# First loads of x from ScalarE's queue, a split last accumulation, and one warming matmul less in a two-layer hybrid decoder trunk

## The chip, the cores and the metric

The kernel runs on one core of one Trainium2 chip. The metric is the device time of one execution in microseconds (us), the median of three runs. Besides that there is one profiled execution with its trace; all rows below are from it. TensorE (PE) does the matmuls, VectorE (DVE) and ScalarE (ACT) the elementwise work, GpSimd (POOL) a few small operations, and SyncE (SP) issues the loads and stores.

## The reference

Two layers work on x of 256 tokens by 1024 channels, in float32. A layer is a token mixer and a feed-forward block, each followed by a layer norm over a scaled residual:

```python
proj = x @ w_in                                     # 1024 -> 4768 columns
q_lat, kv_lat, k_rope, ... = split(proj)            # 384 + 256 + 32 "latent" columns among them
y_rnn = gelu(g_rnn) * rg_lru(causal_dwconv(x_rnn, conv_w, conv_b), ...)   # a scan over the tokens
y_mla = mla_attention(q_lat, kv_lat, k_rope, ...)   # 16 heads, causal
mix = (sigmoid(gate_a) * y_rnn + sigmoid(gate_b) * y_mla) @ w_out
x = layer_norm(ALPHA * x + mix, ln1_g, ln1_b)
h_gate, h_val = split(causal_dwconv(x @ w_up, ffn_conv_w, ffn_conv_b))
x = layer_norm(ALPHA * x + (gelu(h_gate) * h_val) @ w_down, ln2_g, ln2_b)
```

## The kernel before

**Products.** Each float32 operand is split into a rounded part (hi, by ScalarE, L185 or L199) and the rest (lo, by VectorE, L186 or L200). `mm3` (L193) makes three matmuls of a product: hi by hi (L194), hi by lo (L195), lo by hi (L196). TensorE's instructions stand in the order of the program text. The order on every other engine is drawn up by a planner that estimates when each instruction can start; within an engine that order is then fixed.

**Start.** `WARM` = 8 matmuls of a zero tile (L209) run before there is data. `x_block` (L220) loads one or two of the eight 128-channel chunks of x (128 KB each) and splits them; five calls bring all of x. Between them stand the loads of the latent weights, four blocks `lat` of 672 KB (tile `raw`, L156), each split into `wh` and `wl`. All are issued by SP, in program order: x chunk 0 (x0), block 0 in three pieces (168, 168 and 336 KB), x chunk 1 ahead of the third piece, then x chunks 2 and 3 together, block 1 in two pieces of 336 KB, x 4 and 5, block 2, x 6 and 7, block 3; behind them the constants `cst`, the parameters `par` of both layers, the positions `posi` and the next weights (block g0 of the gate projection first). The first accumulation (tile `latp`) takes 12 matmuls of 336 columns for each of the eight chunks. When `par` is there, GpSimd, ScalarE and VectorE make the decay rates from it (tile `lruw`, L329 to L343).

**End.** The down-projection accumulates into `dacc`, for each of two row tiles (128 tokens) two PSUM banks of 512 columns. `finish` (L360) closes row tile 0, starts its layer norm on VectorE (`LayerNorm.tile`, L392), closes the five last chunks of row tile 1 (first half of the columns, then the second), and starts the layer norm of row tile 1. For each half `tile` makes z = ALPHA * residual + sums (L400) and its statistics (L404); then come the mean and variance (L405), the inverse root on GpSimd (L407), two scaling passes (L411, L414) and the stores (L416).

Of the kernel before, what the change touches and what calls it, by code (L numbers as in the profile page):

```python
# [11 lines left out]
F32 = mybir.dt.float32  # L12
# [3 lines left out]
ALU = mybir.AluOpType  # L16

P = 128
# [30 lines left out]
)  # L49
HELD = 4  # L50
WARM = 8
LINE = 256
STEP = 8
KORD = (0, 1, 4, 5, 2, 3, 6, 7)
# [71 lines left out]
def trunk(ctx, tc, x_tok, x_chan, pos, wts, par, lnrow, consts, out):  # L126
    nc = tc.nc
    A = nc.scalar
    V = nc.vector
# [4 lines left out]
    tiny = ctx.enter_context(tc.tile_pool(name="tiny", bufs=2))  # L134
# [8 lines left out]
    def bank(name):  # L143
        return pp.tile([P, 512], F32, tag="pb", name=name)
# [48 lines left out]
    def mm3(o, lh, ll, rh, rl, start, stop):  # L193
        T.matmul(o, lhsT=lh, rhs=rh, start=start, stop=False)  # L194
        T.matmul(o, lhsT=lh, rhs=rl, start=False, stop=False)  # L195
        T.matmul(o, lhsT=ll, rhs=rh, start=False, stop=stop)  # L196

    def split2(hi, lo, src):
        A.activation(hi, src, AF.Copy)  # L199
        V.tensor_tensor(out=lo, in0=src, in1=hi.bitcast(F32), op=ALU.subtract)  # L200
# [6 lines left out]
    spare = bank("spare")  # L207
    for _ in range(WARM):
        T.matmul(spare[:, :P], lhsT=idle, rhs=idle, start=True, stop=True)  # L209
# [9 lines left out]

    def x_block(kc, n):  # L220
        src = x0[kc // 4][:, (kc % 4) * S:(kc % 4 + n) * S]
        nc.sync.dma_start(
            out=src.rearrange("p (c s) -> p c s", c=n),
            in_=x_chan[kc:kc + n].rearrange("c p s -> p c s"),
        )
        hi, lo = (v[:, (kc % 4) * S:(kc % 4 + n) * S] for v in xs[kc // 4])
        split2(hi, lo, src)

    x_block(0, 1)
    latw0.update(latent_weights(  # L230
        0, 0, step=LH, parts=((0, LH), (LH, LATW), (LATW, 2 * LATW)),
        between=lambda: x_block(1, 1)))
    for i in range(1, 4):
        x_block(2 * i, 2)
        latw0.update(latent_weights(0, i, step=LATW if i > 1 else LH,
                                    parts=((0, LATW), (LATW, 2 * LATW))))
# [6 lines left out]
        out=mask[:, P:], in_=mask[:, P:], pattern=[[-1, P]],  # L243
# [108 lines left out]
    def out_last(accs, t, n, wts_of, act_of, hc):  # L352
        for h, c in hc:
            hi, lo = wts_of(c)
            ah, al = act_of(c)
            mm3(accs[t][h], ah[:, t * P:(t + 1) * P], al[:, t * P:(t + 1) * P],
                hi[:, 512 * h:512 * h + 512], lo[:, 512 * h:512 * h + 512],
                False, c == n - 1)

    def finish(ln, accs, n, wts_of, act_of, late):  # L360
        out_last(accs, 0, n, wts_of, act_of, [(h, n - 1) for h in range(2)])
        ln.tile(0, accs)
        hc = [(h, c) for h in range(2) for c in range(n - late, n)]
        out_last(accs, 1, n, wts_of, act_of, hc[:-HELD])
        if not ln.last:
            ln.turn(0)
        out_last(accs, 1, n, wts_of, act_of, hc[-HELD:])
        ln.tile(1, accs)

# [8 lines left out]
    class LayerNorm:  # L378
# [10 lines left out]
            if not last:  # L389
                self.xs = [(slot("xhi", F32R), slot("xlo", F32R)) for _ in range(2)]  # L390

        def tile(self, t, accs):  # L392
            l, last = self.l, self.last
            z = big.tile([P, D], F32, tag="xres", name="z", bufs=4, align_bytes=LINE)
            st = tiny.tile([P, 2, 6], F32, tag="st", name="st")
            mv = tiny.tile([P, 2], F32, tag="mv", name="mv")
            rs = tiny.tile([P, 1], F32, tag="rs", name="rs")
            hs = [slice(512 * h, 512 * h + 512) for h in range(2)]
            for h in range(2):
                V.scalar_tensor_tensor(  # L400
                    out=z[:, hs[h]], in0=self.xres[t][:, hs[h]], scalar=ALPHA, in1=accs[t][h],
                    op0=ALU.mult, op1=ALU.add,
                )
                V.bn_stats(st[:, h], z[:, hs[h]])  # L404
            V.bn_aggr(mv, st.rearrange("p a b -> p (a b)"))  # L405
            V.tensor_scalar(out=rs, in0=mv[:, 1:2], scalar1=EPS, scalar2=None, op0=ALU.add)
            G.tensor_tensor(out=rs, in0=rs, in1=nhalf[:, 0:1], op=ALU.pow)  # L407
            g, b = self.gb
            if last:
                for h in range(2):  # L410
                    V.scalar_tensor_tensor(out=z[:, hs[h]], in0=z[:, hs[h]], scalar=mv[:, 0:1],  # L411
                                           in1=g[:, hs[h]], op0=ALU.subtract, op1=ALU.mult)
                for h in range(2):
                    V.scalar_tensor_tensor(out=z[:, hs[h]], in0=z[:, hs[h]], scalar=rs,  # L414
                                           in1=b[:, hs[h]], op0=ALU.mult, op1=ALU.add)
                    nc.sync.dma_start(out=out[t * P:(t + 1) * P, hs[h]], in_=z[:, hs[h]])  # L416
                return
            nmr = tiny.tile([P, 1], F32, tag="nmr", name="nmr")
            V.scalar_tensor_tensor(out=nmr, in0=mv[:, 0:1], scalar=-1.0, in1=rs,
                                   op0=ALU.mult, op1=ALU.mult)  # L420
            for c in (0, 256):
                V.tensor_scalar(out=z[:, c:c + 256], in0=z[:, c:c + 256], scalar1=mv[:, 0:1],
                                scalar2=rs, op0=ALU.subtract, op1=ALU.mult)
            A.activation(z[:, hs[1]], z[:, hs[1]], AF.Identity, scale=rs, bias=nmr)
            self.res.append(z)
# [84 lines left out]
    ends = (None, None)  # L510
    for l in range(DEPTH):
# [337 lines left out]
        later[0] = False  # L849
        ln = LayerNorm(l, 0, xres, False)  # L850
        finish(ln, oacc, 8, lambda c: ow[c], mer_of, 5)
        tp = [bank("upt") for _ in range(NB)]

# [85 lines left out]
        for j in range(NPAIR - LAG, NPAIR - 1):  # L939
            out_chunk(dacc, j, dw[j], hq[j], (0, 1) if j < NPAIR - LATE else (0,))  # L940
        ln = LayerNorm(l, 1, xres, l == DEPTH - 1)
        finish(ln, dacc, NPAIR, lambda c: dw[c], lambda c: hq[c], LATE)
        if l < DEPTH - 1:
            xs, xres = ln.xs, ln.res
            lat = []
            lacc = [[bank("latp") for _ in range(2)] for _ in range(NT)]
            for i, kc in enumerate(KORD):
                if i == 5:
                    ln.turn(1)
                    ends = ln.ends  # L950
# [113 lines left out]
```

## Time and profile before

| | us |
|---|---|
| median of 3 runs (lowest, highest) | 795.62 (795.12, 796.52) |
| the profiled execution's own time | 796.0 |
| its span, first to last instruction | 794.2 |
| TensorE busy | 781.1 (98% of the span) |
| VectorE busy | 649.7 (82%) |
| ScalarE busy | 508.8 (64%) |
| GpSimd busy | 10.9 (1%) |

Busy time is the time in which an engine has an instruction under way. TensorE's matmuls overlap, so a share of 98% says that it nearly always has work, not how fast it works. The execution's own time holds 1.8 us around the span.

### The profile page before, as it was taken

Reading aid. Unit: us, or ns where it says so; the run is one execution under the profiler, and the core shown is the slowest. Engines: PE = TensorE matmul, PEld = TensorE weight load, DVE = VectorE, ACT = ScalarE, POOL = GpSimd, SP = SyncE. Lnnn points to the kernel's source line nnn. Section 1 sums busy time; section 2 is a strip of 40 time slices with the busy share of each in tenths; the row PEclk is TensorE's granted clock in tenths of the full one; section 3 lists DMA queues with packets and bytes.
Section 4 is the critical chain, followed back from the end, with each engine's and each line's share of the span. In section 5 each row is a group of like instructions: output and inputs, shape, how many; then the busy total and the mean of one; then the engine's idle time right before and its main releaser. Section 6 shows DMA issues by size and latency. Waiting matters only on the chain.

```text
span 794.2 us, 14518 instructions
## 1 busy us (share of the span) xinstructions
PE 781.1 (98%) x5712; PEld 733.8 (92%) x5712; DVE 649.7 (82%) x1260; ACT 508.8 (64%) x910; POOL 10.9 (1%) x27
## 2 busy tenths in 40 slices
PE   8999999999999999999999999999999999999996
PEld 8999899878999999999899999998799999999994
DVE  5998889997699977767877886999877998677765
ACT  5765987783777565555474579688667765556540
POOL 1000000000000000000000000000000000000000
PEclk9999999999999999999999999999999999999998
DMA  8955436525457545535625554563615665646311
GB/s 303 349 198 213 146 113 242 200 68 202 160 205 273 201 174 217 187 123 210 248 73 204 184 178 141 177 214 120 212 62 199 256 228 201 224 163 208 107 54 54
DMA packets 26468, 144.76 MB, mean 182 GB/s; under 512 B 3360, under 2 KB 7072, under 8 KB 11808
## 3 DMA queue, kind: packets, MB, share of 16 engines
q1 hardware_dynamic: 26400, 143.84, 51.2%
q8 instruction: 45, 0.74, 0.4%
q14 instruction: 23, 0.19, 0.1%
HBM read 140.68 MB, written 1.05 MB: 178 GB/s over the span
## 4 chain that ended last, share of the span: by engine, by line
PE 89%; ACT 4%; DVE 3%; DMA 1%; issue 1%; SPq 0%; POOL 0%; DVEq 0%
PE proj L196 16%; PE proj L195 16%; PE proj L194 16%; PE dacc L195 6%; PE dacc L194 6%; PE dacc L196 6%; PE oacc L194 2%; PE oacc L196 2%; PE oacc L195 2%; PE sps L759 2%; PE yps L802 2%; PE ptp L787 1%; PE sps L757 1%; PE upt L196 1%; PE upt L194 1%
## 5 line engine op out<-in xcount | busy, mean ns | idle before, releaser
L196 PE MATMUL proj<-xhi,wl 128*128 128x256 f32 x1216 | 341.0, 280 | 1.3 <-DVE wl L186 1.3
L194 PE MATMUL proj<-xhi,wh 128*128 128x256 f32 x1216 | 341.2, 281 | 0.0
L195 PE MATMUL proj<-xlo,wh 128*128 128x256 f32 x1216 | 341.1, 281 | 0.0
L186 DVE TENSOR_TENSOR wl<-raw,wh 128x1024 fp32r<-128x1024 f32 (+5 forms) x226 | 241.6, 1088 | 47.2 <-ACT wh L185 46.6
L185 ACT ACTIVATE wh<-raw 128x1024 fp32r<-128x1024 f32 (+5 forms) x226 | 209.0, 953 | 99.8 <-PE proj L195 83.8
L196 PEld LDWEIGHTS proj<-xhi,wl 128*128 128x128 f32 x1216 | 229.0, 188 | 1.9 <-DVE wl L186 1.9
L194 PEld LDWEIGHTS proj<-xhi,wh 128*128 128x128 f32 x1216 | 229.1, 188 | 1.4
L195 PEld LDWEIGHTS proj<-xlo,wh 128*128 128x128 f32 x1216 | 228.7, 188 | 1.4
L905 DVE SCALAR_TENSOR_TENSOR u<-proj,par,u 128x255 f32<-128x255 f32 (+1 forms) x176 | 83.5, 479 | 37.6 <-ACT u L902 35.4
L902 ACT ACTIVATE u<-proj,par 128x256 f32<-128x256 f32 x88 | 49.1, 558 | 91.4 <-DVE u L905 71.4
L195 PE MATMUL dacc<-wsl,hh 128*128 128x512 f32 x192 | 75.1, 391 | 0.0
L194 PE MATMUL dacc<-wsh,hh 128*128 128x512 f32 x192 | 75.1, 391 | 0.0
L196 PE MATMUL dacc<-wsh,hl 128*128 128x512 f32 x192 | 75.0, 391 | 0.0
L186 DVE TENSOR_TENSOR wsl<-raw,wsh 128x1024 fp32r<-128x1024 f32 (+2 forms) x66 | 69.8, 1076 | 0.0
L185 ACT ACTIVATE wsh<-raw 128x1024 fp32r<-128x1024 f32 (+2 forms) x66 | 59.7, 938 | 0.0
L196 PEld LDWEIGHTS dacc<-wsh,hl 128*128 128x128 f32 x192 | 36.0, 188 | 7.8
L194 PEld LDWEIGHTS dacc<-wsh,hh 128*128 128x128 f32 x192 | 36.1, 188 | 6.4
L195 PEld LDWEIGHTS dacc<-wsl,hh 128*128 128x128 f32 x192 | 36.1, 188 | 6.2
L199 ACT ACTIVATE hh<-u 128x256 fp32r<-128x256 f32 x48 | 19.6, 408 | 13.7 <-DVE u L913 13.7
L194 PE MATMUL oacc<-wh,mhi 128*128 128x512 f32 x64 | 26.7, 417 | 0.0
L196 PE MATMUL oacc<-wh,mlo 128*128 128x512 f32 x64 | 25.2, 394 | 0.0
L195 PE MATMUL oacc<-wl,mhi 128*128 128x512 f32 x64 | 25.1, 393 | 0.0
(213 smaller groups left out, 1129.1 us busy)
## 6 DMA issues: line engine op xcount, KB each, us to landing
raw<-in_wts SPq DMA_DIRECT2D x114, 1024.0 KB, 4.8
raw<-in_wts SPq DMA_DIRECT2D x8, 832.0 KB, 5.1
gb<-in_lnrow SPq DMA_DIRECT2D x8, 512.0 KB, 7.4
raw<-in_wts SPq DMA_DIRECT2D x4, 672.0 KB, 4.0
raw<-in_wts SPq DMA_DIRECT2D x7, 336.0 KB, 7.1
raw<-in_wts SPq DMA_DIRECT2D x4, 512.0 KB, 4.7
xres<-in_x_tok SPq DMA_DIRECT2D x2, 512.0 KB, 6.0
k<-krot SPq DMA_DIRECT2D x8, 128.0 KB, 2.4
```

What stands on the lines that cost most here:

```text
L185: behind(A.activation(h, w, AF.Copy), after[0])
L186: lo_ins = V.tensor_tensor(out=lo[:, c - a:d - a], in0=w, in1=h.bitcast(F32), op=ALU.subtract)
L194: T.matmul(o, lhsT=lh, rhs=rh, start=start, stop=False)
L195: T.matmul(o, lhsT=lh, rhs=rl, start=False, stop=False)
L196: T.matmul(o, lhsT=ll, rhs=rh, start=False, stop=stop)
L199: A.activation(hi, src, AF.Copy)
L757: T.matmul(sps[:, :P], lhsT=q96[:, h4, :P], rhs=k96[:, h4, :P], start=True, stop=True)
L759: T.matmul(sps[:, P:P + S], lhsT=q96[:, h4, P:], rhs=k96[:, h4], start=True, stop=True)
L787: T.transpose(ptp[:, b * P:(b + 1) * P], sns[hh][:, b * P:(b + 1) * P], ident)
L802: T.matmul(yps[hh * 64:hh * 64 + 64, t * P:S], lhsT=vs[:, hv:hv + 64], rhs=pts[hh][:, 2 * t * P:(2 + t) * P], start=t == 0, stop=t == 1)
L902: ea = A.activation(dst, src, AF.Identity, scale=pcol(l, "fw", 96 + ch), bias=pcol(l, "fb", ch))
L905: ev = V.scalar_tensor_tensor(out=dst[:, k:], in0=src[:, :S - k], scalar=pcol(l, "fw", 48 * (2 - k) + ch), in1=dst[:, k:], op0=ALU.mult, o ...
```

## The change

Three edits. The five loads in `x_block` are issued on ScalarE's queue instead of SP's. In the last layer norm alone, the last `ENDS` = 3 of the five closing chunks of row tile 1's second half are cut in two by columns: columns 512 to 767 go into the old bank, columns 768 to 1023 into a bank of their own, `dend`. `LayerNorm.tile` then makes z of the whole half from the old bank (its last quarter without those three chunks), takes statistics of columns 512 to 767, adds `dend` to the last quarter, and takes that quarter's statistics; the aggregate reads three sets. And `WARM` is 7 instead of 8.

```diff
-WARM = 8
+ENDS = 3
+WARM = 7
...
     def x_block(kc, n):
         src = x0[kc // 4][:, (kc % 4) * S:(kc % 4 + n) * S]
-        nc.sync.dma_start(
+        nc.scalar.dma_start(
...
+    def out_split(accs, t, n, wts_of, act_of, late):
+        ends = bank("dend")[:, :256]
+        for dst, a in ((accs[t][1][:, :256], 512), (ends, 768)):
+            for c in range(n - late, n):
+                hi, lo = (w[:, a:a + 256] for w in wts_of(c))
+                ah, al = (x[:, t * P:(t + 1) * P] for x in act_of(c))
+                mm3(dst, ah, al, hi, lo, a == 768 and c == n - late, c == n - 1)
+        return ends
...
     def finish(ln, accs, n, wts_of, act_of, late):
         out_last(accs, 0, n, wts_of, act_of, [(h, n - 1) for h in range(2)])
         ln.tile(0, accs)
         hc = [(h, c) for h in range(2) for c in range(n - late, n)]
+        if ln.last:
+            out_last(accs, 1, n, wts_of, act_of, hc[:-ENDS])
+            ln.tile(1, accs, out_split(accs, 1, n, wts_of, act_of, ENDS))
+            return
         out_last(accs, 1, n, wts_of, act_of, hc[:-HELD])
-        if not ln.last:
-            ln.turn(0)
+        ln.turn(0)
...
-        def tile(self, t, accs):
+        def tile(self, t, accs, ends=None):
-            st = tiny.tile([P, 2, 6], F32, tag="st", name="st")
+            st = tiny.tile([P, 3, 6], F32, tag="st", name="st")
...
+            cuts = hs if ends is None else [hs[0], slice(512, 768), slice(768, 1024)]
             for h in range(2):
                 V.scalar_tensor_tensor(
                     out=z[:, hs[h]], in0=self.xres[t][:, hs[h]], scalar=ALPHA, in1=accs[t][h],
                     op0=ALU.mult, op1=ALU.add,
                 )
-                V.bn_stats(st[:, h], z[:, hs[h]])
-            V.bn_aggr(mv, st.rearrange("p a b -> p (a b)"))
+                V.bn_stats(st[:, h], z[:, cuts[h]])
+            if ends is not None:
+                V.tensor_tensor(out=z[:, cuts[2]], in0=z[:, cuts[2]], in1=ends, op=ALU.add)
+                V.bn_stats(st[:, 2], z[:, cuts[2]])
+            V.bn_aggr(mv, st[:, :len(cuts)].rearrange("p a b -> p (a b)"))
```

## Rows read from the trace of the kernel before

**Rows 1.** Busy time by stretch: stretch, length, each engine's busy us, clock, DMA share, GB/s.

```profile
0.00:4.50 4.50, 3.45 (x17) 3.45 (x17) 1.08 (x4) 2.18 (x3) 1.24 (x9) 1.00 0.55 137
4.50:8.00 3.50, 2.49 (x15) 2.18 (x14) 1.22 (x4) 1.66 (x4) 0.00 (x0) 1.00 0.94 315
8.00:22.00 14.00, 13.69 (x86) 13.06 (x85) 11.38 (x29) 9.65 (x20) 1.32 (x2) 1.00 1.00 371
...
60.00:130.00 70.00, 67.60 (x563) 66.73 (x562) 60.12 (x88) 53.74 (x80) 0.21 (x2) 1.00 0.52 179
```

**Rows 2.** The chain that ended last, from 0 to 40 us: start, length, what.

```profile
4.06 6.75 DMA raw<-in_wts
10.83 5.16 DMA par<-in_par
16.04 1.33 POOL lruw L329 x2
...
21.00 1.23 DVE wl L186
22.27 0.38 PE proj L196
```

**Rows 3.** Timeline of the first microseconds: start, length, instruction, idle time before and its end.

```profile
0.73 1.28 ACT L199 ACT_TABLE_LOAD   x1 [0.73 <-PEq L1053]
...
1.19 0.90 SPq L156 DMA_DIRECT2D raw<-in_wts  x2
...
2.93 0.42 ACT L199 ACTIVATE xhi<-x 128x256 fp32r<-128x256 f32 x1 [0.91 <-DMA x<-in_x_chan]
...
3.52 0.48 ACT L185 ACTIVATE wh<-raw 128x336 fp32r<-128x336 f32 x1 [0.18 <-DMA raw<-in_wts]
...
4.49 0.59 PE L194 MATMUL latp<-wh,xhi 128*128 128x336 f32 x1
...
7.78 0.42 PE L194 MATMUL latp<-wh,xhi 128*128 128x336 f32 x1 [1.01 <-ACT wh L185]
...
14.08 0.42 PE L195 MATMUL latp<-wl,xhi 128*128 128x336 f32 x1
```

**Rows 4.** DMA issues from 2.5 to 3 us: count, KB, us to landing.

```profile
raw<-in_wts SPq DMA_DIRECT2D x1, 336.0 KB, 4.6
```

**Rows 5.** Lines L209 and L757: ns min/median/max, first and last start.

```profile
L209 PE MATMUL spare<-idle x16: 421/421/579, 1.1 to 4.4; 128*128 128x128 f32 x16
...
L757 PE MATMUL sps<-k,q x64: 272/273/378, 129.8 to 558.3; 96*128 96x128 f32 x64
```

**Rows 6.** Timeline of the end, TensorE and VectorE.

```profile
769.73 0.28 PE L194 MATMUL proj<-xhi,wh 128*128 128x256 f32 x1
769.85 0.28 PE L195 MATMUL proj<-xlo,wh 128*128 128x256 f32 x1
...
784.63 0.74 DVE L414 SCALAR_TENSOR_TENSOR z<-z,rs,gb 128x512 f32<-128x512 f32 x1
...
785.30 0.68 DVE L404 BATCH_NORM_STATS2 st<-z 128x6 f32<-128x512 f32 x1
...
785.96 0.39 PE L195 MATMUL dacc<-wsl,hh 128*128 128x512 f32 x1
...
786.19 0.39 PE L196 MATMUL dacc<-wsh,hl 128*128 128x512 f32 x1
786.62 0.69 DVE L400 SCALAR_TENSOR_TENSOR z<-z,dacc 128x512 f32<-128x512 f32 x1 [0.64 <-PE dacc L196]
787.34 0.69 DVE L404 BATCH_NORM_STATS2 st<-z 128x6 f32<-128x512 f32 x1
788.07 0.21 DVE L405 BATCH_NORM_AGGREGATE mv<-st 128x2 f32<-128x12 f32 x1
```

**Rows 7.** VectorE's groups by shape: count, busy us, mean ns.

```profile
L186 DVE TENSOR_TENSOR wl<-raw,wh 128x512 fp32r<-128x512 f32 x32 | 20.9, 682 | 0.3 <-ACT wh L185 0.2
...
L809 DVE TENSOR_TENSOR mg<-yps,sB 128x256 f32<-128x256 f32 x16 | 6.7, 419 | 1.2 <-PE yps L802 1.2
```

## The prediction

> **What bounds the kernel now.** I read the page first: TensorE is busy for 781.1 of the 794.2 us, so an edit moves the time only where TensorE stands still. Busy time by stretch [rows 1] says where that is. From 0 to 8 us it is busy 5.94 us, part of that with warming matmuls; from 8 to 22 us it lacks 0.3 us; from 60 to 130 us it lacks 2.4 us, which no edit touches; and after its last product (786.6 us) it has 7.6 us of nothing, while the last layer norm and its stores run. The edits lie in the first and the last of these.
>
> The chain that ended last [rows 2] tells what the first pause costs. TensorE's last early stop ends at 22.27 us, when VectorE finishes the lo part of weight block g0 (21.00 to 22.23). VectorE came to that block late, because it first made the decay rates, and those hang on GpSimd at 16.04, which hangs on `par` landing at 15.99. `par` was issued at 10.83, when the second piece of latent block 1 landed (4.06 + 6.75 = 10.81). Counted in order of issue, that piece is the eighth transfer before it: I read this as at most eight transfers in flight. The DMA share is 0.94 and then 1.00 from 4.5 us on, at 371 GB/s from 8 us [rows 1]. So the date of `par` is set by the bytes ahead of it, not by SP's issuing. Stops before that one (7.78 and 14.08, [rows 3]) cost nothing of their own as long as TensorE reaches 22 us with its latent products done.
>
> At the end [rows 6] the chain is TensorE's last product (786.59), then z of the second half (786.62), statistics (787.34), aggregate (788.07), and from there a fixed sequence to the last store. VectorE is idle only from 785.98 to 786.62 there.
>
> **Loads of x on ScalarE.** Removed from SP: five issues at 0.45 us (two took 0.90, [rows 3]), 2.25 us in all. Added to ScalarE: five issues at about the same price, as nearest row. ScalarE stands free from 0.73, but it loads its function table then (1.28 us), under the line of the first activation. The load belongs to that activation, so issues that stand ahead of the activation stand ahead of the load. The five issues wait for no data, the activation does; I take all five to come first. Then: 0.73 + 2.25 + 1.28 = 4.26, hi of x0 to 4.68, hi of the first weights (0.48) to about 5.2. Before, the first products began at 4.49, straight behind the warming matmuls. So TensorE starts some 0.7 us later. Bound below: only x0's issue goes ahead, the table is there at 2.46, before x0 lands (2.93), the weights land 0.45 earlier, and the first product comes at about 4.06.
>
> The fourth and fifth issue may also have to wait for the first landing (eight in flight); queued behind them on ScalarE are the table load and both hi parts: at most 2.93 - 2.55 = 0.4 us more.
>
> The second chunk needs the third piece of block 0. Before, it was issued after 2.5 us, took 4.6 us [rows 4] and let TensorE go on at 7.78. Now SP issues it 0.95 us earlier, but x has a queue of its own that shares the same engines. If the two queues share equally, 672 KB of x have moved when that piece lands, where 256 KB had: 416 KB more, 1.15 us at 371 GB/s. If the transfers start 0.45 us earlier, the piece comes 0.7 us later, and chunk 1 starts at about 8.5, past the late start above (5.2 plus 12 products at 13.69/86 = 0.16 us is 7.1). That is why the late start costs nothing. For chunk 4 (stop at 14.08) the same count is 256 KB more, 0.7 - 0.45 = 0.25 later: 14.3, and four chunks of 1.9 us end at 21.9. The bytes ahead of `par` and g0 are the same, so these come 0.45 earlier and lo of g0 ends at 21.8. Both paths meet at 21.9 instead of 22.27: **-0.4 us**. Bounds: better, if the second queue fills the engines from 2 us on. By 8 us 137 x 4.5 + 315 x 3.5 = 1.72 MB had moved; at 371 GB/s from 2 us it would be 2.23 MB, which is 1.4 us. Worse: 0, if no transfer starts earlier and TensorE's products still end by 22, or a loss by the second rival below.
>
> **One warming matmul less.** It takes 0.43 us of TensorE (eight from 1.05 to 4.49) [rows 3, 5]. Nothing waits for it when data comes at 5.2: 0. What it covers is the clock. The record grants 1.00 throughout, yet these matmuls take 421 ns where a float32 matmul of the same 128 columns later takes 273 [rows 5], so I read them as running at the lower level (1.2 GHz) and the higher (2.4 GHz) as beginning with the first real products. That is priced as a rival.
>
> **The split last accumulation.** TensorE: nine matmuls of 512 columns become eighteen of 256. The pitch of the first is 786.19 - 785.96 = 0.23, of the second 769.85 - 769.73 = 0.12 [rows 6]: 2.16 - 2.07 = 0.1 us more, end at 786.68. The first nine end a microsecond before, at 785.6. VectorE is still on row tile 0's last pass and the first half's statistics then (784.63, 785.30, a pitch of 0.67 for 512 columns), so z of the second half can start at 785.97 and not before. From there by pitches: z to its dependent statistics 0.72 as now, statistics to aggregate 0.73; going from 512 to 256 columns takes 682 - 419 = 0.26 us off an instruction [rows 7]. So the third quarter's statistics start at 786.69, the added sum at 786.69 + 0.67 - 0.26 = 787.10, its statistics at 787.10 + 0.72 - 0.26 = 787.56, the aggregate at 787.56 + 0.73 - 0.26 = 788.03, against 788.07: **-0.04 us**. What VectorE gains by filling its pause it spends on two instructions more. TensorE's extra 0.1 us hides behind this: the added sum could start at 786.71 and starts at 787.10. Statistics of 256 columns have no row. If both cost as much as 512 columns, it is +0.5; if VectorE's order puts row tile 0's last pass behind, z starts at 785.65 and TensorE's end decides: -0.4. I take the rows' slope. The bank `dend` comes from a group last used by the up-projection, 12 us before, so nothing waits for it; the larger statistics tile costs the other layer norms nothing.
>
> **Sum.** -0.4 - 0.04, about -0.4 us. The profiled execution (796.0, span 794.2) would take 795.6 with a span of 793.8; it stands 0.4 above the median, so the median goes from 795.62 to **795.2**. Changes under 0.2% (1.6 us) are about what this measurement cannot tell from none.
>
> **Rivals.**
>
> *The engines fill (faster).* For it: from 0 to 4.5 us the DMA share is 0.55. Against: most of that is time before the first bytes, and the transfers in flight are many. With -1.4 at the start and -0.4 at the end: 793.8.
>
> *TensorE starts cold (slower).* Warming ends at 4.06, the first product comes at 5.2, and the higher clock, which began right with the first products before, may come later. A chunk then takes 3.8 instead of 1.9 us. The first is covered almost whole (5.2 + 3.8 = 9.0 against 8.5); each further one costs 1.9. It decides from the second on: three chunks end the products at 5.2 + 11.4 + 9.5 = 26.1, against 21.9; the stop would be 3.8 us later than now, and the time 799.4. With two chunks (24.2) it is 797.5. For it: the gap of 1.1 us that the edit opens. Against: a gap as long (6.8 to 7.78) was followed by products at full pace. The Trainium skill, TensorE: Matmul & The Clock Gate, What's actually happening, says that the throttled state is the default and activity releases it; by that rule fewer warming matmuls ahead of a gap speak for this rival, and the trace agrees in that the matmuls of the start are the slow ones.
>
> *ScalarE's issues undo the gain (no change).* The five issues and the wait on a landing take all that the freed queue gives; the stop stays at 22.27, the end at -0.04: 795.6. The Trainium skill, ScalarE: Activation LUTs, Table sets: the hidden batching unit, says that a pass puts a load before every activation that needs one; by that rule the table load stands behind x0's issue at least, and the trace has one load, right before the first activation's line. The sum of the late start is then the one above.
>
> *The planner's order changes elsewhere.* Other issue times can change the order on ScalarE and VectorE in the first layer, where TensorE lacks 2.4 us from 60 to 130 us. Losing or doubling that: 792.8 or 797.6.
>
> **Chances.** Forecast 0.50, undone 0.18, engines fill 0.14, cold 0.09, other order 0.09 (half each way). Faster by over 0.2%: most of the engines' case and a third of the other order, 0.14. Slower by over 0.2%: the cold case from two chunks on, and part of the other order, 0.09. Within 0.2%: 0.77. Range: from the engines' case, 793.8, to short of the cold one's two chunks, 797.0.
>
> **What would show it.** Right: ScalarE's table load near 3 us, first product near 5.2, stop on lo of g0 near 21.9, `par` landing near 15.5; at the end z of the second half straight behind the statistics of the first, and the aggregate about 1.35 us behind TensorE's last product (1.48 now, and that product 0.1 later). Wrong: a table load before 2 us, a first product near 4, products of the latent stage at 0.28 us pitch, or a new stop of TensorE between 22 and 130 us.

## The result and the profile after

The changed kernel takes 802.78 us (801.5 to 804.11, four runs) against 795.4 beside it: a ratio of 1.0086, 95% interval 1.0069 to 1.0103. A control later (six more runs) gave 801.16 against 796.49, 1.0059 (1.0047 to 1.0072). So the loss is 5 to 7 us, where the prediction had a gain of 0.4. One execution of a version below (the wider tile alone) took 851.05 us at a mean clock of 0.85; its number there leaves that one out, and its trace, which is of that execution, isn't used.

Its profiled execution has a span of 800.9 us, 6.7 more than before. Where they arise is seen by when the first and the last of the 1216 hi-by-hi products into `proj` start: 24.9 and 776.6 us now, 21.4 and 769.7 before. So 3.5 us are lost ahead of the first projection, 3.4 between, and 0.2 come back at the end.

Busy time by stretch, the same columns as [rows 1]:

```profile
0.00:4.50 4.50, 3.35 (x14) 3.06 (x14) 0.57 (x4) 2.11 (x4) 1.25 (x9) 1.00 0.59 186
4.50:8.00 3.50, 3.19 (x12) 2.66 (x12) 1.35 (x4) 0.82 (x2) 0.00 (x0) 1.00 0.98 313
8.00:22.00 14.00, 11.75 (x66) 11.39 (x67) 10.21 (x29) 8.14 (x18) 0.90 (x2) 0.88 0.91 327
60.00:130.00 70.00, 67.70 (x555) 67.10 (x554) 58.71 (x87) 52.53 (x78) 0.22 (x2) 0.98 0.49 173
92.00:95.40 3.40, 3.40 (x18) 3.40 (x18) 2.79 (x6) 3.37 (x7) 0.00 (x0) 0.51 0.76 251
```

From 8 to 22 us TensorE makes 66 matmuls, where it made 86 [rows 1], and two stretches lie at the lower clock: the mean granted clock is 0.88 in this stretch, and 0.51 from 92.0 to 95.4, which is the level of 1.2 GHz.

The timeline of the start, answering to [rows 3]:

```profile
0.73 1.38 ACTq L223 DMA_DIRECT2D x<-in_x_chan  x3
...
2.14 1.28 ACT L200 ACT_TABLE_LOAD   x1 [2.14 <-issue]
3.67 0.42 ACT L200 ACTIVATE xhi<-x 128x256 fp32r<-128x256 f32 x1 [0.24 <-DMA x<-in_x_chan]
...
4.51 0.65 PE L195 MATMUL latp<-wh,xhi 128*128 128x336 f32 x1
...
6.34 0.45 PE L197 MATMUL latp<-wh,xlo 128*128 128x336 f32 x1
...
6.62 0.32 PE L195 MATMUL latp<-wh,xhi 128*128 128x336 f32 x1
...
6.78 0.31 PE L196 MATMUL latp<-wl,xhi 128*128 128x336 f32 x1
...
7.38 0.32 PE L197 MATMUL latp<-wh,xlo 128*128 128x336 f32 x1
9.07 0.63 ACT L200 ACTIVATE xhi<-x 128x512 fp32r<-128x512 f32 x1 [3.70 <-DMA x<-in_x_chan]
9.61 1.59 ACT L186 ACTIVATE wh<-raw 128x336 fp32r<-128x336 f32 x4
...
10.12 0.65 PE L195 MATMUL latp<-wh,xhi 128*128 128x336 f32 x1 [2.42 <-ACT wh L186]
```

TensorE stops for 2.42 us (1.01 before, at 7.78 [rows 3]). What ends the stop is the hi of block 0's third piece (the first of the four at 9.61). That hi stands behind hi of x chunks 2 and 3 in ScalarE's order, and this one waits 3.70 us for its load. In the kernel before the third piece stood ahead.

The granted clock reads 1.00 up to 8 us, but the first products start at least 0.28 us apart, and only from 6.62 us on 0.15 to 0.16 (in the kernel before from 4.91 on). So the slow pace of the start is not in the mean clock of an execution.

DMA traffic from 2 to 9 us: queue (q1 is SP's, q10 ScalarE's), packets, MB, share of time:

```profile
q1 hardware_dynamic: 826, 1.66, 69.2%
q10 hardware_dynamic: 673, 0.64, 28.4%
...
x<-in_x_chan ACTq DMA_DIRECT2D x3, 256.0 KB, 7.4
```

x gets 45% of the packets, but 28% of the bytes: its packets carry 0.95 KB, SP's 2.0. The load of chunks 2 and 3, issued at about 1.65, takes 7.4 us and lands at 9.05. The third piece (336 KB, issued at about 1.65 too) takes 6.0 us and lands at about 7.6: it lay there for 2 us.

Further on, weight block g0 comes late as well (hi, lo, and its load, issued at 13.18):

```profile
20.88 2.01 ACT L186 ACTIVATE wh<-raw 128x1024 fp32r<-128x1024 f32 x2 [4.42 <-DMA raw<-in_wts]
...
21.98 1.23 DVE L187 TENSOR_TENSOR wl<-raw,wh 128x1024 fp32r<-128x1024 f32 x1 [1.44 <-ACT wh L186]
...
raw<-in_wts SPq DMA_DIRECT2D x1, 1024.0 KB, 7.6
```

In the kernel before this load, issued at 13.25, takes 5.9 us, and its hi starts at 19.25.

The end, VectorE, answering to [rows 6]:

```profile
792.17 0.69 DVE L420 BATCH_NORM_STATS2 st<-z 128x6 f32<-128x512 f32 x1
792.77 0.67 DVE L416 SCALAR_TENSOR_TENSOR z<-z,dacc 128x512 f32<-128x512 f32 x1
793.48 0.43 DVE L420 BATCH_NORM_STATS2 st<-z 128x6 f32<-128x256 f32 x1
793.82 0.40 DVE L422 TENSOR_TENSOR z<-z,dend 128x256 f32<-128x256 f32 x1
794.26 0.43 DVE L423 BATCH_NORM_STATS2 st<-z 128x6 f32<-128x256 f32 x1
794.72 0.24 DVE L424 BATCH_NORM_AGGREGATE mv<-st 128x2 f32<-128x18 f32 x1
```

z of the second half stands straight behind the statistics of the first, as forecast. From it to the aggregate it is 1.95 us (forecast 2.06).

### The profile page after: what moved, and what is told of

The parts are those of the page before. It is cut to its first block, busy times and chain, and to the rows that moved or that the text cites. A ratio compares the mean times of both kernels' runs of the same rounds, so it can differ in the third digit from the quotient of the medians.

```text
span 800.9 us, 14534 instructions
## 1 busy us (share of the span) xinstructions
PE 787.2 (98%) x5719; PEld 739.7 (92%) x5719; DVE 650.1 (81%) x1262; ACT 509.3 (64%) x910; POOL 10.5 (1%) x27
## 3 DMA queue, kind: packets, MB, share of 16 engines
q10 hardware_dynamic: 1104, 1.05, 0.4%
HBM read 140.68 MB, written 1.05 MB: 177 GB/s over the span
```

## The experiments

The theories: **order** (ScalarE's fixed order puts the third piece behind a late load), **address** (the wider statistics tile moves the buffers behind it), **warming** (one matmul less costs clock), and as rivals **bandwidth** (x gets too little on a queue of its own, whatever the order) and the **planner** (a new order of the other instructions). Ratios are to the kernel before, run beside each; they are estimates over all single executions, with a 95% interval, and not quotients of the two medians.

Single executions lie in steps by their mean granted clock. Of the 31 runs of the kernel before beside the last group of experiments, 14 have 0.997 and a median of 795.1 us, 14 have 0.995 and 796.8. Some comparisons below therefore look at times of equal clock.

### One part at a time

**Only the loads of x.** `nc.sync.dma_start` in `x_block` becomes `nc.scalar.dma_start`.

> The loads of x on ScalarE alone. Order theory (ScalarE's fixed order puts hi of x chunks 2 and 3 ahead of the third piece of latent block 0, and that load lands late on a queue of its own): TensorE stops until about 10 us, the clock falls behind that stop, and the time rises by 4 to 5 us, nearly all of the change's loss. Address theory (the wider statistics tile moves the buffers behind it and slows every product a little): only the early stop, 2 to 3 us, and the slow creep from 125 us on is gone. Warming theory (one matmul less sets the clock back): no stop of over 1.5 us and within 1 us of before.

798.46, ratio 1.0038 (1.0024 to 1.0051). TensorE stops for 2.24 us at 10.18, and the projections start at 25.1. The expected stop is there, and with it most of what is lost ahead of the projections. The loss of 2.4 us is what the address theory left for the loads (2 to 3); the order theory's 4 to 5 us, nearly all of the loss, was missed.

**Only the split end**, with the wider statistics tile.

> The split last accumulation alone, with its wider statistics tile. Order theory: the tail is shorter by 0 to 0.3 us and nothing else moves, -0.3 to +0.1 us. Address theory: the tail's gain and a creep of about 2 us over the run, so +1.5 to +2 us.

797.85, ratio 1.0024 (1.0015 to 1.0034): the second part that costs.

**Only `WARM = 7`.**

> Seven warming matmuls alone. Order theory: the first products wait for data as before, within 0.4 us of before. Warming theory: the clock rises one step later, the latent stage loses 1.5 to 3.5 us and the time rises by as much.

797.92, ratio 1.0023 (1.0013 to 1.0032). The edit alone also changes the planner's order on ScalarE and VectorE. The size is what the warming theory forecast, but ScalarE takes a copy of latent sums out of PSUM ahead of hi of g0:

```profile
20.13 0.45 ACT L487 ACTIVATE lat<-latp 128x336 f32<-128x336 f32 x1 [3.09 <-PE latp L196]
20.48 2.00 ACT L185 ACTIVATE wh<-raw 128x1024 fp32r<-128x1024 f32 x2
...
22.84 0.39 PE L196 MATMUL proj<-xhi,wl 128*128 128x256 f32 x1 [0.76 <-DVE wl L186]
```

In the unchanged kernel that hi starts at 18.95. In the changed kernel the order with seven and with eight is the same, so this price is not carried over.

**Control**: the kernel before.

> The kernel before, unchanged, as a control on the same chip. If the four single edits were really slower by 2 us each, this is within 0.1% of the runs of before, 795 to 797 us, with two groups 1.5 to 2 us apart by the mean granted clock (0.997 and 0.995). If the way of running makes the 2 us, this is at 798 too.

795.29, ratio 0.9998 (0.9988 to 1.0007).

The three parts sum to 1.0085, but warming counts there with an order that the whole change doesn't have; loads and split end alone give 1.0062.

### The warming matmul

**Seven and a short eighth** (16 columns), which keeps the kernel before's order:

```diff
-    for _ in range(WARM):
-        T.matmul(spare[:, :P], lhsT=idle, rhs=idle, start=True, stop=True)
+    for n in [P] * 7 + [16]:
+        T.matmul(spare[:, :n], lhsT=idle, rhs=idle[:, :n], start=True, stop=True)
```

> The kernel before with seven warming products of 128 columns and an eighth of 16 columns; the order of the instructions on every engine is the kernel before's, where the run with seven products alone had ScalarE's and VectorE's order changed near 20 us. Planner theory (what seven products cost was the changed order, which puts the first weight's hi behind a wait): 795.1 to 796.2, as the kernel before. Warming theory (the missing columns cost clock at the start): 797 to 798.5, and the stop behind the latent products stays at 0.76 us.

795.7, ratio 1.0001 (0.999 to 1.0012). The planner theory holds: what seven cost was the order, as far as 16 columns more make no difference.

**The changed kernel with `WARM = 8`:**

> The changed kernel with eight warming matmuls; no other instruction moves. Order theory: TensorE has a stop until 10 us either way, so within 0.5 us of the changed kernel (802.8). Warming theory: the clock stays up in more of the runs and it is 1.5 to 2 us faster, about 801.

801.16, ratio 1.006 (1.0047 to 1.0073). Seemingly 1.6 us better than 802.78, but the control of the changed kernel gave 801.16 as well:

> The changed kernel, unchanged, as a control with more runs and a second profile (there are only four runs of it so far). The parts as measured one by one: all of x on ScalarE's queue about 2.4, the moved buffers about 2.4, an additional stretch at half clock about 1.7 in those runs that have it. Sum theory: runs between 799.3 (mean clock 0.997 or above) and 803 (0.994), median 800.5 to 803. Rival (the four runs were high by the chip that they ran on): median below 800.

The sum theory holds: 801.16, ratio 1.0059. And the changed kernel with the third statistics set elsewhere (below) and eight products:

> The changed kernel with its third set of statistics in a slot and with eight warming products. Order of all instructions as in the version with the slot and seven (797.31). If the eighth product itself is worth something at the start (the changed kernel gained 1.6 from it): 795.5 to 796.8. If it is worth nothing and the 1.6 were the scatter of the clock's stretches: 796.9 to 798.8.

798.27, not better than 797.31 with seven. The eighth product is worth nothing that these runs can tell; the 1.6 us between the two results of the changed kernel are not its doing.

### The loads and the order

**x on ScalarE, with hi of the later chunks held behind the last hi of the weight block before:**

```diff
+                last_hi[0] = A.activation(h, w, AF.Copy)
...
-        split2(hi, lo, src)
+        behind(A.activation(hi, src, AF.Copy), last_hi[0])
+        V.tensor_tensor(out=lo, in0=src, in1=hi.bitcast(F32), op=ALU.subtract)
```

> The loads of x on ScalarE, with ScalarE's order held so that hi of x chunks 2 and 3 stands behind block 0's third piece. Order theory: the stop at 10 us shrinks from 2.2 us to under 0.6, the clock stays up behind it, and the run is 1.5 to 2.5 us faster than with the loads on ScalarE alone (798.5), so about 796 to 797. Bandwidth rival (x's own queue gets too little of the engines, whatever the order): the stop stays over 1.5 us, one chunk later, and the time stays at 798 or above.

798.75, ratio 1.0026 (1.0016 to 1.0036). The stop is gone, and the trace shows the third piece landing at 7.58; but later the gain is taken back:

```profile
7.58 0.86 ACT L186 ACTIVATE wh<-raw 128x336 fp32r<-128x336 f32 x2 [2.06 <-DMA raw<-in_wts]
...
8.11 0.42 PE L196 MATMUL latp<-wh,xhi 128*128 128x336 f32 x1 [0.47 <-ACT wh L186]
...
20.71 2.01 ACT L186 ACTIVATE wh<-raw 128x1024 fp32r<-128x1024 f32 x2 [4.24 <-PE latp L198]
...
23.08 0.39 PE L198 MATMUL proj<-xhi,wl 128*128 128x256 f32 x1 [0.76 <-DVE wl L188]
```

The projections start at 21.8, 3.3 us earlier than with the loads alone. But hi of g0 comes at 20.71 (18.95 in the control), TensorE stops at 23.08 for its lo, and this profile has a stretch at half clock near 90 us. The planner had also changed more of VectorE's order than with the loads alone. So order explains the stop at 10 us, but mending it brought back less than these runs can tell: 1.0026 against 1.0038, with intervals that overlap. The order theory's 796 to 797 was met by the three executions with a mean clock of 0.997 (median 796.85); the others lie higher, and the bandwidth rival's stop of over 1.5 us didn't come either.

**Only the first two loads of x on ScalarE**, the three of 256 KB on SP:

```diff
-        nc.sync.dma_start(
+        (nc.scalar if n == 1 else nc.sync).dma_start(
...
```

> The kernel before with only the first two loads of x (one chunk each, 128 KB) issued from ScalarE's queue, and the three larger ones left on SP's. Queue theory (a load of 1-KB rows beside weight loads of longer rows gets the smaller part of the engines, and SP's later issues wait for it): the two small ones land early as in the changed kernel (about 3.7 and 4.4 us), the 256-KB loads are as before, no stop near 10 us; 794.8 to 796.0, within 0.5 of the kernel before. Table-load theory (ScalarE's issues ahead of its table load are what costs): 797 or above.

794.56, ratio 0.9986 (0.9977 to 0.9994): a small gain, where the same edit on all five costs 0.38%. At a mean clock of 0.997 it is 0.45 us (794.54 against 794.99); the rest comes from the steps, for 9 of 11 executions have that clock here and 9 of 28 of the kernel before. What the 0.45 us are the profile doesn't show: its projections start at 21.0, the control's at 20.9. The 256-KB load of chunks 2 and 3 takes 5.5 us here (issued at 2.12, so it lands at 7.6), and there is no stop of TensorE over 0.15 us ahead of the gates.

### The statistics tile and where the buffers lie

`tiny`, the pool of the statistics, lies ahead of those of the weights, the large slots and the small tiles. A wider tile (two buffers, 32 bytes more each) moves the weight halves `wh`, `wl` by 64 bytes, the raw weights, the small tiles and `u` by 256, and the large slots (which hold hi and lo of x) not at all. That is read from the addresses in the built program.

**Only the wider tile**, `[P, 3, 6]`, third set never used; the order of all engines is the kernel before's.

> Only the statistics tile is wider (three sets of six, the third never used); the order on every engine is that of before. Order theory: within 0.3 us of before. Address theory: +1.5 to +2 us, as a creep over the two up-projection stages.

798.7 (six executions), ratio 1.0037 (1.0024 to 1.005). The address theory forecast this, but the tile's own work could cost as much; that is tried below.

**The split end with its three sets in a slot of the large pool**, the regular tile as before:

```diff
-            st = tiny.tile([P, 2, 6], F32, tag="st", name="st")
+            if ends is None:
+                st = tiny.tile([P, 2, 6], F32, tag="st", name="st")
+            else:
+                st = slot("st3")[:, :18].rearrange("p (a b) -> p a b", a=3)
```

> The split last accumulation with its three sets of statistics in a spare large buffer, so that the statistics tile keeps its size and no other buffer moves. Address theory: the creep over the up-projection stages is gone, 0.1 to 0.3 us faster than before, 1.5 to 2 us faster than the split with the wider tile (797.9). Rival (the split itself, or the run): it stays at 797.5 or above.

796.08, ratio 0.9999 (0.999 to 1.0009). The split itself costs nothing and gives nothing that the times can tell. The profiles can: from the start of the last hi-by-hi product into `proj` to the end of the span it is 24.5 us in every version without the split and 24.3 in every one with it.

**The changed kernel with that edit:**

> The changed kernel with one edit: the last row tile's three sets of statistics lie in a slot of the large pool, and the regular statistics tile has two sets again, as before. Order of all instructions as in the changed kernel. Address theory: the wider tile costs its 1.8 to 2.7 us here too; 800.0 to 801.2, and the product pitch of the late projections back at 117.8 ns from 118.9. Rival (the statistics tile costs only beside the early loads of the kernel before): 802 to 803.

797.31, ratio 1.0027 (1.0012 to 1.0041): 3.9 us below the control of the changed kernel, and about what the loads alone cost. That is more than the theory's 1.8 to 2.7: of the 4.2 us between the two profiles, 3.0 lie in the projections and 1.2 ahead of them, where this one has no stretch at half clock.

**The wider tile and an unused tile of 192 bytes**, so that all buffers behind move by 256 bytes together:

```diff
+    tiny.tile([P, 48], F32, tag="pad", name="pad", bufs=1)
```

> The kernel before with the wider statistics tile whose third set is never used, and an unused tile of 192 bytes beside it, so that all buffers behind lie exactly 256 bytes later, instead of the weights' halves 64 bytes later, the raw weights, the small tiles and u 256 bytes later, and the large slots not at all. The order of all instructions is the kernel before's. Address theory as an offset between buffers (the products slow down when the halves of the weights move against the large slots that they are multiplied with): no offset has changed, 795.1 to 796.5, as the kernel before. Rival (the tile itself costs: a longer row that VectorE writes and reads, or any move at all): 797.5 to 799, as with the wide tile alone.

795.32, ratio 1.0 (0.999 to 1.0011).

**An unused tile of 64 bytes at the head of the small pool**: the small tiles and `u` move as with the wider tile, the weights don't.

> The kernel before with an unused tile of 64 bytes at the head of the small pool: krot lies 64 bytes, the small tiles and u 256 bytes later, as with the wide statistics tile, and the weights' halves, the raw weights and the large slots stay. The order of all instructions is the kernel before's. If it is the weights' halves that cost (64 bytes against the large slots): 795.1 to 796.5. If it is the small tiles and u: 797.5 to 799.

796.37, ratio 1.0002 (0.9991 to 1.0012).

**The changed kernel with the 192 bytes:**

> The changed kernel with the same unused tile of 192 bytes, so that all buffers behind the statistics lie 256 bytes later than before the change and none has moved against another. Order of all instructions as in the changed kernel. Offset theory: 796.8 to 798.8, as with the third set in a slot of its own. Rival: 801 to 803, as the changed kernel.

798.36, ratio 1.0039 (1.0022 to 1.0056): 2.8 us below the control by the medians, with the width of the tile unchanged; but the eight executions lie apart, three at 800.9, as high as the control, and five at 796.5 to 798.5. The profiled one is of the three. Its projections take 748.6 us from the first to the last product, one stretch at half clock included; what it loses lies at the start:

```profile
16.04 0.46 PE L197 MATMUL latp<-wl,xhi 128*128 128x336 f32 x1
16.32 0.34 PE L198 MATMUL latp<-wh,xlo 128*128 128x336 f32 x1
16.50 0.32 PE L196 MATMUL latp<-wh,xhi 128*128 128x336 f32 x1
...
L196 PE MATMUL proj<-xhi,wh x1216: 276/280/415, 26.2 to 774.8; 128*128 128x256 f32 x174
```

Up to 16.32 us its products start at least 0.28 apart, only then 0.15, and the projections start at 26.2.

So it is neither the tile's work, nor any move, nor the small tiles: it is where the weights lie. The built program of the last run adds that the raw weights, the small tiles and `u` have the same addresses there as in the changed kernel; the halves lie 192 bytes later and the large slots 256. What is left is the place of the halves or of the raw weights against the large slots, or the halves' own place: they moved by 64 bytes with the wider tile alone, and by a whole 256, on which the raw weights and the slots are aligned, with the 192 bytes beside it. These were not tried apart. The line of the hi-by-hi products into `proj` (ns min/median/max, start of the first and the last) shows the cost, in order for the control of before, the wider tile beside 192 bytes, the split end with the wider tile, the changed kernel with the slot, and the changed kernel's control:

```profile
L194 PE MATMUL proj<-xhi,wh x1216: 276/281/370, 20.9 to 768.7; 128*128 128x256 f32 x174
```

```profile
L195 PE MATMUL proj<-xhi,wh x1216: 276/280/369, 21.5 to 769.1; 128*128 128x256 f32 x174
```

```profile
L195 PE MATMUL proj<-xhi,wh x1216: 274/281/368, 21.5 to 771.0; 128*128 128x256 f32 x174
```

```profile
L195 PE MATMUL proj<-xhi,wh x1216: 276/280/367, 23.8 to 770.9; 128*128 128x256 f32 x174
```

```profile
L195 PE MATMUL proj<-xhi,wh x1216: 274/281/367, 25.0 to 775.1; 128*128 128x256 f32 x174
```

From the first to the last it is 747.8, 747.6, 749.5, 747.1 and 750.1 us. The granted clock is 1.00 in all five over that time. The moved weights cost 1.7 to 1.9 us in the kernel before and 3.0 in the changed one, and no stop of TensorE is longer. By the starts in the traces, 1.7 of the 1.9 and 2.7 of the 3.0 lie in the products into `proj`, all of which read the halves; the products of the up-projection into `upt`, which read large slots alone, take the same. With the loads of x on ScalarE some halves also lie in other buffers of their pool (seen in the built programs), so the two prices need not be equal.

### The stretches at half clock, and the parts that held

Eight products of zeros fill the two stops of 0.99 us that the last gate chunk of layer 0 has in the kernel before (at 85.97 and 87.36 us), beside the split end with its statistics in a slot:

```diff
+                fill = 4 if l == 0 and c == 7 else 0
+                for _ in range(fill):
+                    T.matmul(ps[:, :P], lhsT=idle, rhs=idle, start=True, stop=True)
...
+                    for _ in range(fill if m == 0 else 0):
+                        T.matmul(o[:, :P], lhsT=idle, rhs=idle, start=False, stop=False)
```

> The split end with its statistics in a slot of their own (as in the run of that version, 796.08), and in layer 0 eight products of the idle tile (zeros, 128 columns) in the two stops of the last gate chunk: four ahead of its first product, four between its first and second, added into the open sum. About 0.2 us each against two stops of 0.99 us, so no product behind them should start later. Order of all other instructions as in that version. Clock theory: the two groups of times of the kernel before (795.1 with a mean clock of 0.997, 797.0 with 0.995) are one stretch at half clock behind these two stops; filled, no run shows it, nearly all runs lie at 0.997 or above, median 794.3 to 795.2, about 0.6 below the kernel before beside it. Rival (the stretch has another cause, such as the load on the chip): both groups stay, median 795.7 to 796.3. Second rival: the eight products delay the chunk, each of 0.2 us on the path, up to 1 us slower in the upper group.

795.23 (794.6 to 795.84, 11 runs), ratio 0.9993 (0.9984 to 1.0001). All 11 runs have a mean clock of 0.997 or above, where 18 of 28 of the kernel before beside it have 0.995. The clock theory holds; the gain in the median is on the edge of what can be told.

**Together**: this, and the first two loads of x on ScalarE.

> What held together: the first two loads of x from ScalarE's queue and the three larger ones from SP's, the split end with its statistics in a slot, eight warming products, and the eight products of zeros in the two stops of layer 0's last gate chunk. If the gains add (about 0.7 from the loads at equal clock, 0 to 0.1 from the split, and only the upper group of times): 793.8 to 794.8, 0.9 to 1.5 below the mean of the kernel before beside it. Rival (the filled stops move the low stretch elsewhere, or the start's gain is taken back behind the latent products): 794.9 to 796.

794.21 (793.88 to 794.76), ratio 0.998 (0.9971 to 0.9988). This beats both kernels. Stretches around the last gate chunk, columns as above, first in the run with 64 bytes in the small pool (the stops as they are), then in this one:

```profile
84.50:86.50 2.00, 0.68 (x3) 0.48 (x4) 2.00 (x4) 2.00 (x5) 0.00 (x0) 1.00 0.00 0
86.50:89.90 3.40, 3.40 (x18) 3.40 (x18) 2.79 (x6) 3.40 (x8) 0.00 (x0) 0.50 0.49 139
```

```profile
84.50:86.50 2.00, 1.90 (x15) 1.71 (x16) 2.00 (x3) 2.00 (x5) 0.00 (x0) 1.00 0.00 0
86.50:89.90 3.40, 3.40 (x32) 3.40 (x31) 2.78 (x6) 3.40 (x8) 0.00 (x0) 1.00 0.60 196
```

Eighteen products in 3.4 us against 32: at a pitch of 0.12 us, 1.7 us are lost in the one stretch, which is the step between the runs with 0.997 and 0.995.

## Why the prediction was wrong

**The loads, -0.4: the sign was wrong.** The step that failed is "the piece comes 0.7 us later, and chunk 1 starts at about 8.5". The piece did come (about 7.6), but the sum took it that ScalarE takes it as it lands. The planner writes ScalarE's order from its own idea of the landings, and it put hi of chunks 2 and 3 first. Chunk 1 went on at 10.12, and the projections started at 23.8 in the changed kernel with the slot against 20.9 in the control: +2.9 us, half a microsecond more than the loads alone cost between medians (798.46 - 796.1 = 2.4). A second step of the sum failed behind it: "The bytes ahead of `par` and g0 are the same, so these come 0.45 earlier and lo of g0 ends at 21.8". g0's load took 7.6 us instead of 5.9, and its lo ended at 23.2. TensorE's late products cover that in the changed kernel; with the order held it is what TensorE stops for at 23.08. The prediction had an order rival, but put it at 60 to 130 us and not at the edited place.

**"If the two queues share equally"** was wrong for bytes, and nearly right for packets: 673 and 826 packets, 0.64 and 1.66 MB. The Trainium skill, DMA: Bandwidth & Descriptors, Queues, rings and completion order, says that each engine goes round the queues with work packet by packet; the trace is near that (45% of the packets), if its packets are the page's, of several descriptors each, which no run shows. Here the load of short rows beside loads of longer ones became slower: 7.4 us against 5.5 for the same 256 KB on SP (4.8 in the kernel before). How much of the loss is this share and how much the order is not priced apart: the run that held the order gave back behind 20 us much of what it won at 10.

**The table load and the late start.** Three issues, not five, came ahead of the load (2.14 to 3.42), and the first product came at 4.51, not at 5.2. So the start wasn't late at all, and "as long as TensorE reaches 22 us with its latent products done" broke at the stop for chunk 1 and the lower clock behind it. `par` did come earlier (GpSimd goes on at 14.92, 16.04 before [rows 2]; forecast some 0.45), but this was no longer what TensorE waited for.

**The split end, -0.04: the mechanism was right, the size too small.** Every step came in the order forecast, and the end is 0.2 us shorter in the profiles. Of the 0.16 that the forecast lacks, 0.11 are the steps from z to the aggregate (1.95 us against 2.06); the aggregate stands 1.16 us behind TensorE's last product, where 1.35 was forecast. The ratio of 0.9999 can't tell 0.04 from 0.2.

**"The larger statistics tile costs the other layer norms nothing": wrong where it was not looked for.** It costs the layer norms nothing; it moves the weights, and the products lose 1.7 to 3.0 us. Of all terms this is the one that no row of before could show. The Trainium skill, SBUF — State Buffer, Who interferes with whom, says that TensorE and ScalarE never wait on anyone. Whether a wait is behind the loss here no run shows; with equal order the products take 747.1 us at the one address and 750.1 at the other. What in the products slows is not shown.

**One warming matmul less, 0: right** as far as the runs can tell (795.7 with the order kept). That the higher clock begins with the first real products is right for the profile that the prediction read (0.16 apart from 4.91 us on) and not in general: in the control of the same kernel that begins at 7.11, in the changed kernel at 6.62. Over all profiles, with seven as with eight, it lies between 4.8 and 7.4, except in the one that follows.

**Cold start, the rival for slower: it came in part.** In the changed kernel a stretch at half clock came behind the stop of 2.42 us, and not behind a late first product. It is in both profiles of the changed kernel (10.0 to 13.4 and 10.3 to 13.8), absent in the one with the slot and in the one with eight warming products, though both have the stop, and it costs some 1.2 us of start (25.0 against 23.8). In the profile of the changed kernel with the 192 bytes the rival came as written: the first 32 products start at least 0.28 us apart. Its projections started at 26.2, where the sum for three slow chunks had 26.1. That the two numbers meet is luck, for that sum had no stop in it.

Loads 0.38% and moved weights 0.24 to 0.37% make 1.0062 to 1.0075, between the two results of the change (1.0059 and 1.0086). Why the four executions of the first result lie 1.6 us above the six of the control stays open. Stretches at half clock don't account for it: two of the four have a mean clock of 0.997 and 0.998 and took 801.5 and 802.91 us, the control's one with 0.997 took 799.52. A slow start, as in the run with the 192 bytes, would not show in the mean clock; only one of the four has a trace, and its start is no later than the control's (24.9 against 25.0).

## What to carry to other kernels

- A transfer's landing is only half of a wait. Where a planner fixes an engine's order, look at what the edit does to that order, at the edited place first.
- A buffer that grows moves what lies behind it. Keep scratch that one place needs out of shared small pools, or fill them up so that everything moves alike, and measure the size change by itself.
- Stops of 1 us on TensorE can cost nearly as much again behind them (here 1.7 us behind two of 0.99, in some executions); fill them with products of zeros where nothing waits for them.

## What was not expected of the hardware

- Products of the same kind, order and clock take 747.1 or 750.1 us from the first to the last by where their operands lie: 0.4% for a shift of the split weights by 64 bytes (and of the raw weights by 256) against the large slots.
- Two stops of 0.99 us, 0.4 us apart, bring a stretch of 3.4 us at half clock in some runs of the same program and not in others, which makes two groups of times 1.7 us apart. With the stops filled all 22 runs have a mean clock of 0.997 or above.
- The products of zeros take 1.06 and 1.05 us in stops of 0.99, and still nothing starts later: from the gate product ahead of the first stop to the one behind it 1.26 us, and to the one behind the second 1.39 more, in the kernel before and with the stops filled.
